# Three u tiles side by side at the start of a hybrid GLA and S5 block, with their weights laid out by the host

## The chip, the cores and the metric

The program runs on one core of a Trainium2 chip. The metric is the device time of one execution in microseconds (us); the time before is the median of three runs. The engines are TensorE (PE; its weight loads are PEld), VectorE (DVE), ScalarE (ACT), GpSimd (POOL) and SyncE (SP), which here only starts transfers.

## What is computed

One decoder block on 512 tokens and 16 meta tokens of width 1024. RMSNorm, then one wide projection `w_in` whose columns feed two mixers: gated linear attention (q, k, v, r, a) and a grouped diagonal state-space layer S5 (u). Gates mix both, then follow an output projection and a squared-ReLU MLP, each with a norm around it. The prologue, which the change is about, computes `u` and the normed input:

```python
xn = rmsnorm(h, g_mix_pre[l])          # h * rsqrt(mean(h*h) + EPS) * g
proj = xn @ w_in[l]
a_low = proj[..., R_END:A_END]
u = proj[..., A_END:U_END]             # 1024 columns, 8 tiles of 128
```

## The kernel before

Every product is made of three passes in float32r: an operand is split into a rounded part (`hi`, by ScalarE) and a remainder (`lo`, by VectorE), and TensorE adds hi x hi, hi x lo and lo x hi into one bank of PSUM. The contraction over 1024 is in 8 steps `k` of 128, so one weight tile of 128 columns against one token group is 24 matmuls. The tokens are cut into two halves of 256 and 272 (`HALVES`).

The norm's factor per token isn't known when the first bytes are in. So the prologue multiplies the *raw* tokens, scaled by the norm vector g alone (`taken_raw`: `rh` by ScalarE, `rl` by VectorE, from the transposed tokens `xT`, which the host provides in two pieces `x_cols0` and `x_cols1`), and applies the factor to the results (`u_took`, `scale_rows`). Tiles 0 to 4 of u go this way; the words below call their weights w0 to w4.

- Five warm-up matmuls (`busy(5)`) run on constants.
- ScalarE's queue starts the transfers of g and of the first quarters (two k) of w0 and w1, then loads its function table. SP's queue starts slices of x and the rest of w0 and w1 in the order of the list at L475, then the second half of x, `ab`, w2, the tokens by rows (`xt`) and the further weights. An issue may wait for the landing of an earlier transfer; the transfers of one queue go in order.
- `side_by_side` multiplies w0 and w1 against the first half, k by k, w0's three passes and then w1's; then the same against the second half. Then comes w2 alone against the first half, with `spread(0)` before its fourth k, w2 against the second half, w3 with `spread(1)` before its fourth k, w3 and w4.
- `squared` and `rooted` make the factor `xrs` from the tokens by rows. `spread` turns it into rows with a few small float32 matmuls; `rows_of` (ScalarE) copies these out. All that VectorE does next hangs on it: `u_took` of the first results, `scaled` (x times factor), `low` (remainder of the normed tokens, `xl`), in between the remainders of w3 and w4, and at the end `wa`, the weights of `a_low`.
- Then `low_rank` is the first product on the normed tokens (`mm<-xh,wa`); from there on the dense tiles follow one by one, each with weights prepared two slots ahead.

In the prologue the orders of TensorE, VectorE and ScalarE are those of the code (`keep_in_program_order`). Weight buffers (`wraw`, `whi`, `wlo`) are three deep.

Of the kernel before, what the change touches and what calls it, by code (L numbers as in the profile page):

```python
# [44 lines left out]
NBLK = GRP // GB  # L45

C_Q, C_K, C_V, C_R, C_A, C_U, C_ZG, C_ZS = 0, 512, 1024, 2048, 3072, 3088, 4112, 5136


@with_exitstack  # L50
def hybrid_block(ctx: ExitStack, tc: tile.TileContext, io, out: bass.AP):
# [406 lines left out]
    V.memset(ones, 1.0)  # L458
    g8 = mk(pxt, [P, KT], tag="g8")
    nc.scalar.dma_start(g8, io["g_cols"])  # L460
    xT = mk(pxt, [P, KT, NT], tag="xT")
    rh, rl = (mk(pxt, [P, KT, LINE + SEQ], F32R, tag=t)[:, :, :NT] for t in ("rh", "rl"))
    raws, xts, loaded = [mk(wp, [P, KT, P], tag="wraw", bufs=3) for _ in range(2)], {}, None

# [3 lines left out]
    def first_w(queue, i, k, n):  # L468
        return queue.dma_start(raws[i][:, k : k + n], w_in[k * P : (k + n) * P, C_U + i * P : C_U + (i + 1) * P].rearrange("(k p) n -> p k n", p=P))

    first_w(nc.scalar, 0, 0, 2)
    held = first_w(nc.scalar, 1, 0, 2)
    with tc.issue_after(held.ins):
        S.activation(warm, warm, AF.Sqrt)
    for i, k, n in (("x", 0, 1), ("x", 1, 1), (0, 2, 2), ("x", 2, 2), (1, 2, 2), ("x", 4, 2), (0, 4, 4), (1, 4, 4), ("x", 6, 2)):  # L475
        with behind():
            if i == "x":
                loaded = nc.sync.dma_start(xT[:, k : k + n, :256], io["x_cols0"][:, k : k + n])
            else:
                loaded = first_w(nc.sync, i, k, n)  # L480
    idle = bank()
# [12 lines left out]
    early = []  # L494
    for kind, i in (("h", 0), ("h", 4), ("a", 0), ("u", 2), ("x", 0), ("x", 1), ("x", 2), ("x", 3), ("x", 4), ("u", 3), ("u", 4), ("w", 0), ("g", 0), ("u", 5), ("c", 0), ("u", 6), ("u", 7)):
        with behind():
            if kind == "x":
                loaded = x_load(i)
            elif kind == "h":
                loaded = nc.sync.dma_start(xT[:, i : i + 4, 256:], io["x_cols1"][:, i : i + 4])  # L500
            elif kind == "a":
                loaded = nc.sync.dma_start(ab, io["a_step"])
            elif kind == "w":
                wraw = mk(pg, [P, KT, 16], tag="waraw")
                loaded = nc.sync.dma_start(wraw, w_in[:, C_A : C_A + 16].rearrange("(k p) n -> p k n", p=P))
            elif kind == "g":
                wgu = scratch()[:96].rearrange("p a b -> p (a b)")
                loaded = nc.sync.dma_start(wgu, io["w_gates"])
            elif kind == "c":
                for dst, src in ((CA, io["c_cols"][0]), (CB, io["c_cols"][1]), (BA, io["b_cols"][0])):  # L510
                    loaded = nc.sync.dma_start(dst.rearrange("p g h -> p (g h)"), src)
            else:
                loaded, raw = raw_w(w_in[:, C_U + i * P : C_U + (i + 1) * P])
                raws.append(raw)
# [73 lines left out]

    def side_by_side(ws, q, pss):
        a, b = HALVES[q]  # L590
        for k in range(KT):
            for (hi, lo), ps in zip(ws, pss):
                for i, (w, t) in enumerate(((hi, rh), (hi, rl), (lo, rh))):
                    PE.matmul(ps[:, : b - a], w[:, k], t[:, k, a:b], start=(k == 0 and i == 0), stop=(k == KT - 1 and i == 2))

# [4 lines left out]
    uts = [u_tile() for _ in range(3)] + [mk(qc, [P, T8, NCK], tag=f"ut{i}") for i in (3, 4)]  # L600
    busy(5)
    w0, w1 = (tuple(mk(wp, [P, KT, P], F32R, tag=t, bufs=3) for t in ("whi", "wlo")) for _ in range(2))
    for k in range(KT):
        taken_raw(k, 0)
        for w, raw in zip((w0, w1), raws):
            if k in (0, 2):
                split_part(w, raw, slice(k, k + 2))
            elif k == 4:
                split_part(w, raw, slice(k, KT))
    firsts = bank("mm"), bank()  # L610
    side_by_side((w0, w1), 0, firsts)
    for k in range(KT):
        taken_raw(k, 1)
    last = {0: bank("mm"), 1: bank("mm")}
    side_by_side((w0, w1), 1, (last[0], last[1]))
    w2_ = split_w(raws[2])
    squared(0)
# [5 lines left out]
    squared(2)  # L623
    pair2, spreads = bank("mm"), []
    raw_product(w2_, 0, pair2, (3, lambda: spreads.append(spread(0))))
    rows_of(0, spreads[0])
# [9 lines left out]
    high(0, range(0, 4))  # L636
    last[2] = bank()
    raw_product(w2_, 1, last[2])
    low(0, (0, 2))
    raw_product(w3, 0, pair2[:, 256:], (3, lambda: spreads.append(spread(1))))  # L640
    w4_hi = split_w_hi(raws[4])
# [3 lines left out]
    low(0, (4, 6))  # L645
    last[3] = bank()
    raw_product(w3, 1, last[3])
    last[4] = bank()
# [1352 lines left out]
def laid_out(np, given):  # L2001
# [11 lines left out]
    tokens = np.concatenate([a["x"][0], a["meta_tokens"]]).T.reshape(8, P, NT).transpose(1, 0, 2)  # L2013
    rows["x_cols0"], rows["x_cols1"] = tokens[:, :, :256], tokens[:, :, 256:]
    rows["w_gates"] = np.concatenate([a["w_gate_up"][0]] * 6)
    rows["g_cols"] = a["g_mix_pre"][0].reshape(8, P).T
    return {**{name: a[name] for name in _INS}, **rows}
# [26 lines left out]
```

## Time and profile before

| what | value |
|---|---|
| median of 3 runs | 860.62 us (860.51 to 862.09) |
| the profiled execution's own time | 861.4 us |
| its span, first to last instruction | 859.7 us |
| TensorE busy | 849.5 us, 99% |
| VectorE busy | 680.2 us, 79% |
| ScalarE busy | 465.0 us, 54% |

Times in the profile are us from the first instruction. A row of the timeline has start, length, engine, line, operation and tiles (`out<-in`); in brackets stands how long the engine was idle before it and who released it. The length of a matmul is modelled and longer than its spacing, so spacings are read from starts. L61, L66 and L79 are helpers through which all matmuls and the ordered instructions go; the tile's name tells them apart.

### The profile page before, as it was taken

What the parts mean: (1) busy time and instruction counts of PE and PEld (TensorE: products, weight loads), DVE (VectorE), ACT (ScalarE), POOL (GpSimd) and SP (SyncE); (2) the same over time, 40 slices, a digit from 0 to 9 for tenths busy, and PEclk for the clock granted to TensorE, in tenths of its full rate; (3) what the DMA queues carried; (4) which work ended last, traced back from release to release, by engine and by line L of the source; (5) the groups of instructions that cost most, each with busy time, mean ns of one, the idle gap of its engine ahead of it and who ended that gap; (6) DMA issues with size and microseconds to landing.
All of it is one profiled execution on the core that took longest, in us unless ns stands there. A gap on an engine that the chain in (4) does not pass through costs nothing.

```text
span 859.7 us, 13744 instructions
## 1 busy us (share of the span) xinstructions
PE 849.5 (99%) x4952; PEld 726.6 (85%) x4952; DVE 680.2 (79%) x1264; ACT 465.0 (54%) x816; POOL 151.1 (18%) x265
## 2 busy tenths in 40 slices
PE   9999999999999999999999999999999999999996
PEld 8998899898988888888888889988888888888885
DVE  6999889988787499856888788667666777688886
ACT  7677466676764455335454466433222246885763
POOL 1123120140303222341121421011121100000001
PEclk9999999999999999999999999999999999999998
DMA  9887775566465856977788896498989967866564
GB/s 313 194 281 225 224 143 146 147 174 168 115 156 154 241 156 149 257 202 270 233 271 266 270 294 196 147 323 291 360 262 343 352 223 234 278 195 196 172 199 144
DMA packets 172491, 192.66 MB, mean 224 GB/s; under 512 B 18648, under 2 KB 127352, under 8 KB 172424
## 3 DMA queue, kind: packets, MB, share of 16 engines
q1 hardware_dynamic: 145040, 109.66, 45.1%
q0 software_dynamic: 25408, 77.93, 27.2%
q10 hardware_dynamic: 1976, 4.20, 1.6%
q8 instruction: 39, 0.64, 0.3%
q14 instruction: 28, 0.23, 0.1%
HBM read 149.52 MB, written 42.24 MB: 223 GB/s over the span
## 4 chain that ended last, share of the span: by engine, by line
PE 52%; issue 2%; POOL 1%; DMA 1%; DVE 1%; ACT 0%; DVEq 0%; POOLq 0%
PE mm L61 36%; PE sm L61 16%; DMA qi<-qd 1%; POOL M L1178 0%; PE sm L66 0%; POOL td L1277 0%; DVE c L1964 0%; POOL qd L1250 0%; DVE c L1938 0%; POOL qi L1448 0%; DVE gl L1450 0%; DVEq L2040 0%; ACT gh L164 0%; DMA kpad<-krow 0%; DVE ff_r L150 0%
## 5 line engine op out<-in xcount | busy, mean ns | idle before, releaser
L164 ACT ACTIVATE whi<-wraw 128x1024 fp32r<-128x1024 f32 x81 | 85.8, 1059 | 181.1 <-PE mm L61 177.6
L179 DVE TENSOR_TENSOR wlo<-wraw,whi 128x1024 fp32r<-128x1024 f32 x81 | 99.1, 1225 | 79.0 <-ACT whi L164 77.2
L61 PE MATMUL mm<-xh,whi 128*128 128x512 f32 (+2 forms) x464 | 158.5, 342 | 0.0
L61 PE MATMUL mm<-xh,wlo 128*128 128x512 f32 (+2 forms) x464 | 155.5, 335 | 0.0
L61 PE MATMUL mm<-xl,whi 128*128 128x512 f32 (+2 forms) x464 | 155.4, 335 | 0.0
L61 PE MATMUL mm<-hh,whi 128*128 128x512 f32 (+1 forms) x272 | 100.9, 371 | 0.0
L61 PE MATMUL mm<-hl,whi 128*128 128x512 f32 (+1 forms) x272 | 100.8, 371 | 0.0
L61 PE MATMUL mm<-hh,wlo 128*128 128x512 f32 (+1 forms) x272 | 100.8, 371 | 0.0
L61 PEld LDWEIGHTS mm<-xh,whi 128*128 128x128 f32 x464 | 87.4, 188 | 9.7 <-issue 1.0
L61 PEld LDWEIGHTS mm<-xh,wlo 128*128 128x128 f32 x464 | 87.4, 188 | 9.0
L61 PEld LDWEIGHTS mm<-xl,whi 128*128 128x128 f32 x464 | 87.4, 188 | 8.4
L1881 DVE TENSOR_TENSOR wlo<-wraw,whi 128x1024 fp32r<-128x1024 f32 x56 | 68.4, 1223 | 21.4 <-ACT whi L1877 21.3
L61 PE MATMUL sm<-wlo,fh 128*128 128x512 f32 x192 | 74.9, 390 | 0.0
L61 PE MATMUL sm<-whi,fl 128*128 128x512 f32 x192 | 74.8, 390 | 0.0
L61 PE MATMUL sm<-whi,fh 128*128 128x512 f32 x192 | 74.8, 389 | 0.0
L1877 ACT ACTIVATE whi<-wraw 128x1024 fp32r<-128x1024 f32 x56 | 58.7, 1050 | 15.5 <-PE mm L61 11.7
L61 PEld LDWEIGHTS mm<-hh,whi 128*128 128x128 f32 x272 | 51.3, 189 | 8.8
L61 PEld LDWEIGHTS mm<-hh,wlo 128*128 128x128 f32 x272 | 51.3, 189 | 8.7
L61 PEld LDWEIGHTS mm<-hl,whi 128*128 128x128 f32 x272 | 51.3, 189 | 8.6
L164 ACT ACTIVATE fh<-f 128x512 fp32r<-128x512 f32 x48 | 30.2, 629 | 36.8 <-PE sm L61 23.0
L61 PE MATMUL mm<-gl,whi 128*128 128x512 f32 x128 | 50.0, 390 | 0.1
L61 PE MATMUL mm<-gh,whi 128*128 128x512 f32 x128 | 49.9, 390 | 0.0
(490 smaller groups left out, 1863.2 us busy)
## 6 DMA issues: line engine op xcount, KB each, us to landing
wraw<-in_w_ff_dram SPq DMA_DIRECT2D x56, 512.0 KB, 7.5
wraw<-in_w_in_dram SPq DMA_DIRECT2D x46, 512.0 KB, 5.6
w2raw<-in_w_ff_dram POOLq DMA_DIRECT2D x16, 1024.0 KB, 9.0
t2d<-w2t POOLq DMA_DIRECT2D x16, 1024.0 KB, 6.3
wraw<-t2d SPq DMA_DIRECT2D x32, 512.0 KB, 4.2
wraw<-in_w_glu_dram SPq DMA_DIRECT2D x16, 512.0 KB, 5.2
M<-kpad POOLq DMA_DIRECT2D x64, 64.0 KB, 2.6
wraw<-in_w_o_gla_dram SPq DMA_DIRECT2D x8, 512.0 KB, 7.4
```

The costliest lines, as they stand in the source:

```text
L61: ins = nc.tensor.matmul(*args, **kw)
L164: return S.activation(dst, src, AF.Copy, scale=scale)
L179: V.tensor_sub(lo, raw, f32(hi))
L1877: halved = S.activation(bh, raw, AF.Copy)
L1881: V.tensor_sub(bl, raw, f32(bh))
```

## The change

- `FIRST = 3`: the first three tiles run side by side in both halves. For each k the pass is now the outer loop and the tile the inner one. w2's separate products go away, and so does its separate split.
- The host lays the three tiles out as `w_first`, for each tile one line of 4 KB per partition; a transfer of two k moves 1 KB per partition, one of four k 2 KB, where it moved pieces of 512 B out of `w_in`.
- The norm vector and the first slice of x are one array `g_x_cols` and one transfer into one tile `gx`; g's own transfer goes. `xT` and `g8` are views of that tile.
- The list of first transfers has w2 in it, x comes as 1, 1, 2 and 4 k, and the second half of x as 2 and 6 k (it was 4 and 4).
- Four warm-ups in place of five.
- `spread(0)` now stands before the sixth k of the three tiles' second half, and `spread(1)` before the third k of w3's second half.

```diff
     pxt = pool("pxt", stack=sx, padded=True)
     ones = mk(pxt, [P, 256], tag="ones")
     V.memset(ones, 1.0)
-    g8 = mk(pxt, [P, KT], tag="g8")
-    nc.scalar.dma_start(g8, io["g_cols"])
-    xT = mk(pxt, [P, KT, NT], tag="xT")
+    gx = mk(pxt, [P, KT + KT * NT], tag="gx")
+    g8, xT = gx[:, :KT], gx[:, KT:].rearrange("p (k t) -> p k t", t=NT)
     rh, rl = (mk(pxt, [P, KT, LINE + SEQ], F32R, tag=t)[:, :, :NT] for t in ("rh", "rl"))
-    raws, xts, loaded = [mk(wp, [P, KT, P], tag="wraw", bufs=3) for _ in range(2)], {}, None
+    raws, xts, loaded = [mk(wp, [P, KT, P], tag="wraw", bufs=3) for _ in range(FIRST)], {}, None
 
     def behind():
         return tc.issue_after(loaded.ins) if loaded else ExitStack()
 
     def first_w(queue, i, k, n):
-        return queue.dma_start(raws[i][:, k : k + n], w_in[k * P : (k + n) * P, C_U + i * P : C_U + (i + 1) * P].rearrange("(k p) n -> p k n", p=P))
+        return queue.dma_start(raws[i][:, k : k + n], io["w_first"][i][:, k : k + n])
 
     first_w(nc.scalar, 0, 0, 2)
     held = first_w(nc.scalar, 1, 0, 2)
     with tc.issue_after(held.ins):
         S.activation(warm, warm, AF.Sqrt)
-    for i, k, n in (("x", 0, 1), ("x", 1, 1), (0, 2, 2), ("x", 2, 2), (1, 2, 2), ("x", 4, 2), (0, 4, 4), (1, 4, 4), ("x", 6, 2)):
+    for i, k, n in (("x", 0, 1), (2, 0, 2), ("x", 1, 1), (0, 2, 2), (1, 2, 2), ("x", 2, 2), (2, 2, 2), (0, 4, 4), ("x", 4, 4), (1, 4, 4), (2, 4, 4)):
         with behind():
-            if i == "x":
-                loaded = nc.sync.dma_start(xT[:, k : k + n, :256], io["x_cols0"][:, k : k + n])
+            if i != "x":
+                loaded = first_w(nc.sync, i, k, n)
+            elif k:
+                loaded = nc.sync.dma_start(xT[:, k : k + n, :256], io["x_cols0"][:, k - 1 : k - 1 + n])
             else:
-                loaded = first_w(nc.sync, i, k, n)
+                loaded = nc.sync.dma_start(gx[:, : KT + 256], io["g_x_cols"])
...
     early = []
-    for kind, i in (("h", 0), ("h", 4), ("a", 0), ("u", 2), ("x", 0), ("x", 1), ("x", 2), ("x", 3), ("x", 4), ("u", 3), ("u", 4), ("w", 0), ("g", 0), ("u", 5), ("c", 0), ("u", 6), ("u", 7)):
+    for kind, i in (("h", 0), ("h", 2), ("a", 0), ("x", 0), ("x", 1), ("x", 2), ("x", 3), ("x", 4), ("u", 3), ("u", 4), ("w", 0), ("g", 0), ("u", 5), ("c", 0), ("u", 6), ("u", 7)):
         with behind():
             if kind == "x":
                 loaded = x_load(i)
             elif kind == "h":
-                loaded = nc.sync.dma_start(xT[:, i : i + 4, 256:], io["x_cols1"][:, i : i + 4])
+                loaded = nc.sync.dma_start(xT[:, i : 3 * i + 2, 256:], io["x_cols1"][:, i : 3 * i + 2])
...
-    def side_by_side(ws, q, pss):
+    def side_by_side(ws, q, pss, within=None):
         a, b = HALVES[q]
         for k in range(KT):
-            for (hi, lo), ps in zip(ws, pss):
-                for i, (w, t) in enumerate(((hi, rh), (hi, rl), (lo, rh))):
-                    PE.matmul(ps[:, : b - a], w[:, k], t[:, k, a:b], start=(k == 0 and i == 0), stop=(k == KT - 1 and i == 2))
+            if within and k == within[0]:
+                within[1]()
+            for i, (part, t) in enumerate(((0, rh), (0, rl), (1, rh))):
+                for w, ps in zip(ws, pss):
+                    PE.matmul(ps[:, : b - a], w[part][:, k], t[:, k, a:b], start=(k == 0 and i == 0), stop=(k == KT - 1 and i == 2))
 
...
-    busy(5)
-    w0, w1 = (tuple(mk(wp, [P, KT, P], F32R, tag=t, bufs=3) for t in ("whi", "wlo")) for _ in range(2))
+    busy(4)
+    ws_ = [tuple(mk(wp, [P, KT, P], F32R, tag=t, bufs=3) for t in ("whi", "wlo")) for _ in range(FIRST)]
     for k in range(KT):
         taken_raw(k, 0)
-        for w, raw in zip((w0, w1), raws):
+        for w, raw in zip(ws_, raws):
             if k in (0, 2):
                 split_part(w, raw, slice(k, k + 2))
             elif k == 4:
                 split_part(w, raw, slice(k, KT))
-    firsts = bank("mm"), bank()
-    side_by_side((w0, w1), 0, firsts)
+    firsts, pair2, spreads = (bank("mm"), bank()), bank("mm"), []
+    side_by_side(ws_, 0, (*firsts, pair2[:, :256]))
     for k in range(KT):
         taken_raw(k, 1)
-    last = {0: bank("mm"), 1: bank("mm")}
-    side_by_side((w0, w1), 1, (last[0], last[1]))
-    w2_ = split_w(raws[2])
     squared(0)
     squared(1)
     V.tensor_copy(tri, trif)
@@ -621,8 +622,8 @@
     rooted(slice(0, 2))
     work(1.3)
     squared(2)
-    pair2, spreads = bank("mm"), []
-    raw_product(w2_, 0, pair2, (3, lambda: spreads.append(spread(0))))
+    last = {0: bank("mm"), 1: bank("mm"), 2: bank()}
+    side_by_side(ws_, 1, (last[0], last[1], last[2]), (5, lambda: spreads.append(spread(0))))
     rows_of(0, spreads[0])
     for i in range(2):
         u_took(firsts[i][:, :256], uts[i], 0, True)
@@ -634,17 +635,15 @@
     rooted(slice(2, TT + 1))
     scaled(0, range(6, 8))
     high(0, range(0, 4))
-    last[2] = bank()
-    raw_product(w2_, 1, last[2])
     low(0, (0, 2))
-    raw_product(w3, 0, pair2[:, 256:], (3, lambda: spreads.append(spread(1))))
+    raw_product(w3, 0, pair2[:, 256:])
+    last[3] = bank()
+    raw_product(w3, 1, last[3], (2, lambda: spreads.append(spread(1))))
...
-    last[3] = bank()
-    raw_product(w3, 1, last[3])
...
     tokens = np.concatenate([a["x"][0], a["meta_tokens"]]).T.reshape(8, P, NT).transpose(1, 0, 2)
-    rows["x_cols0"], rows["x_cols1"] = tokens[:, :, :256], tokens[:, :, 256:]
+    rows["x_cols0"], rows["x_cols1"] = tokens[:, 1:, :256], tokens[:, :, 256:]
     rows["w_gates"] = np.concatenate([a["w_gate_up"][0]] * 6)
-    rows["g_cols"] = a["g_mix_pre"][0].reshape(8, P).T
+    rows["g_x_cols"] = np.concatenate([a["g_mix_pre"][0].reshape(8, P).T, tokens[:, 0, :256]], axis=1)
+    rows["w_first"] = a["w_in"][0][:, C_U : C_U + FIRST * P].reshape(KT, P, FIRST, P).transpose(2, 1, 0, 3)
```

SP's queue, from the program's start: before (`xT` is x, `wraw_49` is w0, `wraw_50` is w1, `wraw_52` is w2).

```order
L478 DMA xT_46_149<-in_x_cols0_dram 128x256 x2
L469 DMA wraw_49_152<-in_w_in_dram 128x2x128
L478 DMA xT_46_149<-in_x_cols0_dram 128x2x256
L469 DMA wraw_50_153<-in_w_in_dram 128x2x128
L478 DMA xT_46_149<-in_x_cols0_dram 128x2x256
L469 DMA wraw_49_152<-in_w_in_dram 128x4x128
L469 DMA wraw_50_153<-in_w_in_dram 128x4x128
L478 DMA xT_46_149<-in_x_cols0_dram 128x2x256
L500 DMA xT_46_149<-in_x_cols1_dram 128x4x272 x2
L502 DMA ab_20_116<-in_a_step_dram 128x192
L170 DMA wraw_52_170<-in_w_in_dram 128x8x128
```

And with the change (`gx` is x, `wraw_48`, `49` and `50` are w0, w1 and w2; ScalarE's queue starts the first quarters of w0 and w1 in both).

```order
L482 DMA gx_45_147<-in_g_x_cols_dram 128x264
L469 DMA wraw_50_152<-in_w_first_dram 128x256
L480 DMA gx_45_147<-in_x_cols0_dram 128x256
L469 DMA wraw_48_150<-in_w_first_dram 128x256
L469 DMA wraw_49_151<-in_w_first_dram 128x256
L480 DMA gx_45_147<-in_x_cols0_dram 128x2x256
L469 DMA wraw_50_152<-in_w_first_dram 128x256
L469 DMA wraw_48_150<-in_w_first_dram 128x512
L480 DMA gx_45_147<-in_x_cols0_dram 128x4x256
L469 DMA wraw_49_151<-in_w_first_dram 128x512
L469 DMA wraw_50_152<-in_w_first_dram 128x512
L502 DMA gx_45_147<-in_x_cols1_dram 128x2x272
```

All of w2 now goes ahead of the second half of x (`x_cols1`), where it came behind it; a row of 128x256 is 128 KB.

TensorE at the start of the first half: before, the warm-ups and the first k (`whi_74`, `wlo_75` of w0, `whi_76`, `wlo_77` of w1).

```order
L61 MATMUL sm_51_166<-ones_44_145 128x256 x5
L61 MATMUL mm_78_250<-rh_47_150,whi_74_218 128x256
L61 MATMUL mm_78_250<-rl_48_151,whi_74_218 128x256
L61 MATMUL mm_78_250<-rh_47_150,wlo_75_219 128x256
L61 MATMUL sm_79_251<-rh_47_150,whi_76_220 128x256
L61 MATMUL sm_79_251<-rl_48_151,whi_76_220 128x256
L61 MATMUL sm_79_251<-rh_47_150,wlo_77_221 128x256
```

And with the change (`whi_73`, `75` and `77` are those of w0, w1 and w2, `wlo_74`, `76` and `78` their remainders).

```order
L62 MATMUL sm_51_167<-ones_44_145 128x256 x4
L62 MATMUL mm_79_256<-rh_46_148,whi_73_216 128x256
L62 MATMUL sm_80_257<-rh_46_148,whi_75_218 128x256
L62 MATMUL mm_81_258<-rh_46_148,whi_77_220 128x256
L62 MATMUL mm_79_256<-rl_47_149,whi_73_216 128x256
L62 MATMUL sm_80_257<-rl_47_149,whi_75_218 128x256
L62 MATMUL mm_81_258<-rl_47_149,whi_77_220 128x256
L62 MATMUL mm_79_256<-rh_46_148,wlo_74_217 128x256
L62 MATMUL sm_80_257<-rh_46_148,wlo_76_219 128x256
L62 MATMUL mm_81_258<-rh_46_148,wlo_78_221 128x256
```

The third row of every k now needs w2, and the first remainder `wlo` is wanted in the seventh place.

TensorE around `spread(0)`: before, inside w2 alone (`mm_86`) against the first half.

```order
L61 MATMUL mm_86_393<-rh_47_150,whi_82_366 128x256
L61 MATMUL mm_86_393<-rl_48_151,whi_82_366 128x256
L61 MATMUL mm_86_393<-rh_47_150,wlo_83_368 128x256
L61 MATMUL sm_87_403<-ident_3_78,xrs_66_202 128x128 x2
L61 MATMUL mm_86_393<-rh_47_150,whi_82_366 128x256
L61 MATMUL mm_86_393<-rl_48_151,whi_82_366 128x256
L61 MATMUL mm_86_393<-rh_47_150,wlo_83_368 128x256
```

And with the change, inside the three tiles' second half (`mm_84`, `mm_85`, `sm_86`).

```order
L62 MATMUL mm_84_370<-rh_46_148,wlo_74_217 128x272
L62 MATMUL mm_85_371<-rh_46_148,wlo_76_219 128x272
L62 MATMUL sm_86_372<-rh_46_148,wlo_78_221 128x272
L62 MATMUL sm_87_418<-ident_3_78,xrs_65_201 128x128 x2
L62 MATMUL mm_84_370<-rh_46_148,whi_73_216 128x272
L62 MATMUL mm_85_371<-rh_46_148,whi_75_218 128x272
L62 MATMUL sm_86_372<-rh_46_148,whi_77_220 128x272
```

In front of it stand 45 matmuls of 272 columns of that half, where there were the whole half of two tiles (48) and 9 of w2.

## Rows read from the trace of the kernel before

**Rows 1.** The page, part 1: busy time, share, instructions of TensorE.
```profile
PE 849.5 (99%) x4952; PEld 726.6 (85%) x4952; DVE 680.2 (79%) x1264; ACT 465.0 (54%) x816; POOL 151.1 (18%) x265
```

**Rows 2.** Waits of TensorE, whole run: us in total, times, longest us.
```profile
PE sm L61 <- DVE xss L517: 1.3, 1, 1.3
...
```

**Rows 3.** Timeline of TensorE, first half; then one window: us, busy, clock, DMA.
```profile
1.31 4.16 PE L61 MATMUL sm<-ones 128*128 128x256 f32 x10 [1.31 <-DVE xss L517]
...
10.40 0.39 PE L61 MATMUL sm<-rh,whi 128*128 128x256 f32 x1 [0.32 <-ACT whi L79]
10.62 0.28 PE L61 MATMUL sm<-rl,whi 128*128 128x256 f32 x1
11.12 0.39 PE L61 MATMUL sm<-rh,wlo 128*128 128x256 f32 x1 [0.22 <-DVE wlo L79]
...
11.86 0.28 PE L61 MATMUL sm<-rh,whi 128*128 128x256 f32 x1
...
13.55 0.28 PE L61 MATMUL mm<-rh,whi 128*128 128x272 f32 x1
...
5.20:13.55 8.35, 7.63 (x50) 1.00 1.07 345
```

**Rows 4.** Timeline of ScalarE, where it waits for transfers in the prologue.
```profile
4.73 0.42 ACT L79 ACTIVATE whi<-wraw 128x256 fp32r<-128x256 f32 x1 [0.57 <-DMA wraw<-in_w_in_dram]
5.63 0.42 ACT L79 ACTIVATE whi<-wraw 128x256 fp32r<-128x256 f32 x1 [0.49 <-DMA wraw<-in_w_in_dram]
...
9.72 0.63 ACT L79 ACTIVATE whi<-wraw 128x512 fp32r<-128x512 f32 x1 [0.80 <-DMA wraw<-in_w_in_dram]
...
12.27 3.42 ACT L79 ACTIVATE rh<-xT,g 128x272 fp32r<-128x272 f32 x8 [0.60 <-DMA xT<-in_x_cols_dram]
15.60 1.04 ACT L79 ACTIVATE whi<-wraw 128x1024 fp32r<-128x1024 f32 x1
```

**Rows 5.** VectorE behind spread(0): one window, then its last row.
```profile
21.86:37.32 15.46, 15.36 (x36) 1.00 1.01 233
...
37.03 0.29 DVE L79 TENSOR_TENSOR wa<-waraw,wa 128x128 fp32r<-128x128 f32 x1
```

**Rows 6.** Timeline of TensorE around spread(0), spread(1) and at low_rank.
```profile
20.54 0.61 PE L61 MATMUL sm<-ident,xrs 128*128 128x128 f32 x4
20.90 0.37 PE L61 MATMUL mm<-rh,whi 128*128 128x256 f32 x1
...
26.60 0.28 PE L61 MATMUL mm<-rh,wlo 128*128 128x256 f32 x1
27.02 1.00 PE L61 MATMUL sm<-ident,xrs 128*128 128x128 f32 x6
27.95 0.39 PE L61 MATMUL mm<-rh,whi 128*128 128x256 f32 x1
...
38.52 0.28 PE L61 MATMUL mm<-xh,wa 128*32 128x256 f32 x1
```

**Rows 7.** Transfers in 7 to 8, 11 to 12 and 16 to 17 us.
```profile
DMA packets 627, 0.31 MB, mean 314 GB/s; under 512 B 19, under 2 KB 627, under 8 KB 627
...
DMA packets 363, 0.39 MB, mean 388 GB/s; under 512 B 5, under 2 KB 363, under 8 KB 363
...
DMA packets 119, 0.42 MB, mean 422 GB/s; under 512 B 16, under 2 KB 16, under 8 KB 119
```

**Rows 8.** Timeline of VectorE, the remainder of w1's second half.
```profile
10.38 0.69 DVE L79 TENSOR_TENSOR wlo<-wraw,whi 128x512 fp32r<-128x512 f32 x1 [0.74 <-ACT whi L79]
```

**Rows 9.** Waits of VectorE from 21.5 to 104 us, all of them.
```profile
DVE wlo L79 <- ACT whi L79: 0.5, 2, 0.3
DVE wgr L79 <- ACT wgr L79: 0.2, 1, 0.2
```

**Rows 10.** Timelines of VectorE and TensorE at 82 us.
```profile
81.11 1.20 DVE L79 TENSOR_TENSOR wlo<-wraw,whi 128x1024 fp32r<-128x1024 f32 x1
...
82.65 0.39 PE L61 MATMUL mm<-xh,wlo 128*128 128x512 f32 x1
```

More of the change, by code (lines that the diff above doesn't have):

```diff
@@ L45 @@
 NBLK = GRP // GB
+FIRST = 3
 C_Q, C_K, C_V, C_R, C_A, C_U, C_ZG, C_ZS = 0, 512, 1024, 2048, 3072, 3088, 4112, 5136
```

## The prediction

> **What bounds the kernel now.** I read the page first, then the waits of TensorE, then the start of the run on each engine. TensorE is busy for 849.5 of 859.7 us [rows 1], and the list of what TensorE waited for over the whole run has four entries, the longest the 1.3 us shown, the others at most 0.3 [rows 2]. So the time falls only if TensorE gets through the prologue sooner, and if nothing later makes it wait for what was gained.
>
> In the prologue the first token half runs from 5.20 to 13.55 us, 8.35 us [rows 3]. Its 48 matmuls of 256 columns are spaced 0.113 us when nothing is missing (15 of them from 11.86 to 13.55), which would be 5.4 us. The rows at 10.40 and 11.12 name what is missing: the rounded weights `whi` and their remainder `wlo`. Behind them stands the transfer: ScalarE sat idle for 0.80 us until the second half of weight tile 1 had landed, and took it up at 9.72 [rows 4]. So TensorE waits for ScalarE, which waits for bytes. Behind the first half TensorE is dense, but VectorE is close behind it: from 21.86 to 37.32 us VectorE works 15.36 of 15.46 us without a break and ends with `wa` [rows 5], which TensorE wants at 38.52 [rows 6].
>
> **The change part by part.** *Three tiles in the first half.* The first half grows from 48 to 72 matmuls and the 24 that w2 had later go away. The work is the same; the point is to fill holes with it. Without the change, the equal point (all 72 done) is 13.55 plus 24 matmuls of w2. At 0.113 these are 2.7 us: 16.3 us.
>
> When are they done with the change? The weights' second halves are asked for in the order w0, x, w1, w2, and one row of TensorE's order behind the first matmul of each k needs w2. Ahead of the end of w2's second half the queues carry 2564 KB (ScalarE's 256, and 2308 on SP's queue by the order shown above; 128x256 elements are 128 KB). Before, 1792 KB were in by 9.72 and 2592 KB by 12.27 [rows 4]. On that line, (2564-1792)/800 x 2.55 + 9.72 = 12.2 us: the late end.
>
> *The host's layout.* All of w's rows were 512 B; now they are 1 and 2 KB. What row size is worth in this prologue can be read from three stretches of one us [rows 7]: 314 GB/s in a stretch of 627 packets averaging about 0.5 KB, 388 in one of 363 of about 1.1 KB, 422 in one of 119 of about 3.5 KB. I anchor at the weights of tile 1 that ScalarE took at 5.63, behind 640 KB [rows 4]; the change has 644 KB by the like point, which I leave at 5.6. The other 1920 KB (1.966 MB) then take 4.7 us at 422, 5.1 at 388, 6.3 at 314: landing at 10.3, 10.7 or 11.9. I take 10.7, since the pieces are 1 and 2 KB and half of them are still slices of x in 1 KB rows; the ends are 10.3 and 12.2.
>
> The Trainium skill speaks against this part: in "DMA: Bandwidth & Descriptors", section Specifications, it puts the smallest transfer for line rate at 512 B, so that longer rows would bring nothing. By that rule the sum keeps the 12.2. The trace does not agree: 314 against 388 GB/s.
>
> From landing to the end of the half: ScalarE rounds w2 (0.63, the row at 9.72), VectorE subtracts (0.69 [rows 8]), with about 0.13 for three hand-overs; the first matmul behind a wait is spaced 0.22 (10.40 to 10.62 [rows 3]), and 27 more of 0.113 are 3.05. Together 4.7 us, so the half ends at 15.4 against 16.3: **0.9 us gained**. The same sum from the landing at 9.72, with 18 matmuls in place of 27, gives 13.4 where the trace has 13.55.
>
> *Weights innermost* (`side_by_side`): the remainder `wlo` is wanted as the seventh of nine and no longer as the third of three, which covers VectorE's 0.69; I count it only in that wait.
>
> *The norm vector with x, ScalarE's list one DMA shorter.* ScalarE gets to its table load one DMA issue earlier, but then waits for the first slice and for weights, as at 4.73 and 5.63 [rows 4]. Nothing on the path; a loss is excluded only as far as the first slice (4 KB longer) doesn't land later than the weights behind it.
>
> *One warm-up less* takes 0.83 us (4.16 for five [rows 3]) out of the time ahead of the first product. The first weights are rounded at 5.15 (4.73 + 0.42), so the four that are left, done at about 4.7, end in idle time: price nothing, unless the clock suffers (below).
>
> *spread(1)* moves behind 21 more matmuls. There TensorE's spacing was 0.42 ahead of the six small matmuls and 0.93 over them, where four cost 0.36 at 20.54 [rows 6]: some 0.7 us of waiting for `xrs`, now covered by products. And `w2`'s split leaves ScalarE's and VectorE's lists between the halves and goes into the first half.
>
> **Where it stalls next.** The three-tile second half puts spread(0) 45 matmuls of 272 columns in, 45 x 0.1234 = 5.55 us behind 15.4: at **21.0** in place of 20.54. Its input is in time: before, ScalarE's path from the first rounding of the second half (12.27) to spread(0) took 8.3 us with 1.04 for w2 in it [rows 4, 6]; without w2 it is 7.2, and the last slices land near 10.7 + 1.114 MB at 388 GB/s = 13.6, so it ends by 20.8 even if it began only then. But `rows_of(0)` hangs on spread(0), and all of VectorE's unbroken stretch on that: `wa` comes 16.8 us behind spread(0) (37.32 less 20.54 [rows 5, 6]), at 37.8. TensorE alone would be there at 38.5 - 0.9 - 0.7 = 36.9. So VectorE sets it, and of 1.6 us **0.7** are left.
>
> VectorE stays on the heels of TensorE. It has three idle spots up to 104 us, 0.5 us behind `whi` in two and 0.2 behind `wgr` [rows 9]. I give back 0.5 of these 0.7, where ScalarE stands behind products that TensorE now has earlier, and leave 0.2 for a weight's landing, which the change doesn't hurry. At 82.65 TensorE wants a `wlo` that VectorE finished at 82.31 (81.11 + 1.20): slack 0.34, less 0.05 for the hand-over [rows 10]. VectorE, 0.45 later at spread(0) and 0.5 recovered, is there about 0.05 earlier: TensorE can be at most 0.35 earlier. That is the tightest place I found. **Net: about 0.4 us faster.** The profiled execution took 861.4 (its span and 1.7 around it), so 861.0; it lay 0.8 above the median of 860.62, which becomes 860.2.
>
> **The rivals.** *Late bytes: the layout buys nothing* (the change doesn't do what it says). For it: the stretches of long rows all lie later in the run than those of short ones, so the time of the run could be what differs. w2 lands at 12.2, 1.5 later than in my sum: the half ends at 16.9, spread(0) at 22.5, and the same chain through VectorE makes 1.1 us of loss: 861.7. It turns into a loss from a landing at about 11.1.
>
> *VectorE isn't the bound after all*: were its stretch to start or run sooner, TensorE's own 1.6 us stay: 859.0, and 858.6 with a landing at 10.3. Against it: the 15.36 of 15.46 us, in an order that the change keeps.
>
> *Slower: TensorE stays at its slow level through the first half.* The warm-ups ran 0.42 us for each of ten records of 256 columns [rows 3], where the four records of 128 columns at 20.54 took 0.36 together [rows 6], 0.09 each: some half pace, the 1.2 of the two levels 1.2 and 2.4 GHz. From 5.20 to 13.55 the granted clock is 1.00 [rows 3]. With one of five taken away the rise could come late. If all 72 matmuls went at 0.213, the half would end at 5.2 + 15.3 = 20.5, 5.1 us behind my 15.4: 865.3. It decides only if the low level lasts past the w2 wait, near 12 us; before that the matmuls wait for bytes anyhow. Against it: full spacing stands right behind the w1 waits, from 11.86 on, after a stretch that was no denser than the new one.
>
> The Trainium skill, "TensorE: Matmul & The Clock Gate", Part 1, says that the default state is throttled and that activity releases the throttle, which is this rival's mechanism. The trace agrees that the warm-ups ran at the low level; no run here yet shows fewer of them.
>
> **How the numbers follow.** My forecast, a gain of 0 to 1.1 us (landing 10.3 to 11.1, VectorE as the bound): 0.57, time 860.2. Late bytes, 861.7: 0.2. TensorE's own gain, 859.0: 0.12. Slow level, 865.3: 0.07. Something unlisted: 0.04, either way. Two tenths of a per cent, about what a measurement can tell from no change, are 1.7 us. The forecast and the late bytes lie within it; of the third case half lies beyond. Faster 0.10, same 0.79, slower 0.11. The range takes in the first three cases, and the runs of one kernel, which spread from 860.51 to 862.09: 858.8 to 862.0.
>
> **What would show it.** In the profile after: `whi` of the third tile taken up behind a wait for its weights near 10.7, and the 72nd matmul near 15.4; spread(0) near 21.0; TensorE waiting for `wlo` of w3 or for `wa` around 25 and 37.8, where it didn't wait before; the first `mm<-xh,wa` near 37.8; a short wait for `wlo` near 82. It would be wrong if the third tile's weights land before 10 or after 11.5, if spread(0) doesn't hold VectorE, if matmuls past 12 us are spaced 0.22, or if a later wait swallows what the prologue gave.

## The result and the profile after

The changed kernel takes 863.55 us (median of 8 runs, 862.98 to 865.36) where the kernel before takes 861.47 beside it (8 runs): the ratio is 1.0027, with a 95% interval from 1.0017 to 1.0036. It is **2.1 us slower**, and outside the range that I gave (858.8 to 862.0). The profiled execution took 863.5, so it stands for the median; its span is 861.8, where before it was 859.7.

From the page of the changed kernel the line of busy times, and the head of the list of what TensorE waited for (us in total, times, longest), which answer to [rows 1] and [rows 2]:

```profile
PE 849.8 (99%) x4950; PEld 726.5 (84%) x4950; DVE 680.2 (79%) x1266; ACT 465.2 (54%) x818; POOL 151.1 (18%) x265
```

```profile
PE mm L62 <- ACT whi L80: 1.7, 3, 0.6
PE sm L62 <- DVE xss L519: 1.3, 1, 1.3
PE mm L62 <- DVE wlo L80: 0.8, 1, 0.8
```

TensorE's work is the same (849.5 and 849.8 us busy). The waits for `whi` and `wlo`, the two halves of a weight, come to 2.5 us, where before had some 0.5. One of them, 0.54 us at 8.54, counts for nothing as long as the next, at 11.86, ends on a landing; the others lie at two places, which the next views show. First, ScalarE at the end of the first token half, and TensorE behind it (start us, us, engine, line, operation, out<-in; in brackets the idle time ahead and what ended it):

```profile
9.01 0.49 ACT L80 ACTIVATE rh<-gx 128x256 fp32r<-128x256 f32 x1
10.78 0.51 ACT L80 ACTIVATE rh<-gx 128x256 fp32r<-128x256 f32 x1 [1.27 <-DMA gx<-in_x_cols_dram]
11.20 1.65 ACT L80 ACTIVATE whi<-wraw 128x512 fp32r<-128x512 f32 x3
```

```profile
10.98 0.28 PE L62 MATMUL mm<-rh,wlo 128*128 128x256 f32 x1
11.86 0.38 PE L62 MATMUL mm<-rh,whi 128*128 128x256 f32 x1 [0.61 <-ACT whi L80]
12.38 0.38 PE L62 MATMUL sm<-rh,whi 128*128 128x256 f32 x1
12.90 0.38 PE L62 MATMUL mm<-rh,whi 128*128 128x256 f32 x1
...
17.08 0.41 PE L62 MATMUL mm<-rh,whi 128*128 128x272 f32 x2
```

ScalarE is idle from 9.5 to 10.78, and what ends it is no weight but x: slices 4 to 7, which the change asks for as one DMA of 512 KB ahead of the second halves of w1 and w2. Behind it stand four roundings in a row, and TensorE gets its three `whi` at 11.86, 12.38 and 12.90. The first half is over at **17.08**; the equal point of before was worked out as 16.3, and I had forecast 15.4. Here 0.8 us are lost.

Second, the end of the second token half, on TensorE, ScalarE and VectorE:

```profile
22.64 0.61 PE L62 MATMUL sm<-ident,xrs 128*128 128x128 f32 x4
...
26.30 0.28 PE L62 MATMUL sm<-rh,wlo 128*128 128x272 f32 x1
27.11 0.38 PE L62 MATMUL mm<-rh,whi 128*128 128x256 f32 x1 [0.53 <-ACT whi L80]
27.34 0.28 PE L62 MATMUL mm<-rl,whi 128*128 128x256 f32 x1
28.38 0.39 PE L62 MATMUL mm<-rh,wlo 128*128 128x256 f32 x1 [0.76 <-DVE wlo L80]
...
31.73 0.93 PE L62 MATMUL sm<-ident,xrs 128*128 128x128 f32 x6
...
40.70 0.28 PE L62 MATMUL mm<-xh,wa 128*32 128x256 f32 x1
```

```profile
26.00 1.06 ACT L80 ACTIVATE whi<-wraw 128x1024 fp32r<-128x1024 f32 x1 [1.03 <-PE mm L62]
```

```profile
27.09 1.23 DVE L80 TENSOR_TENSOR wlo<-wraw,whi 128x1024 fp32r<-128x1024 f32 x1 [0.80 <-ACT whi L80]
```

ScalarE wants to round tile 3's weights and waits 1.03 us **for TensorE**: there are three buffers each of `whi` and `wlo`, and w0, w1 and w2 hold all three until the three-tile second half is nearly over. Only then do the rounding (1.06) and the subtraction (1.23) follow, and TensorE stands still for most of 26.4 to 28.4, some 1.85 us. spread(1), at 31.73, has no wait ahead of it any more.

`mm<-xh,wa`, the first product of `low_rank`, starts at 40.70 where it was 38.52 [rows 6]: 2.18 later, and the span is 2.1 longer. So all of the loss is in the first 41 us: 0.8 from the first half, 1.85 from tile 3's split, and some 0.4 back where spread(1) waited before.

### The profile page after: what moved, and what is told of

The parts are those of the page before. It is cut to its first block, busy times and chain, and to the rows that moved or that the text cites. A ratio compares the mean times of both kernels' runs of the same rounds, so it can differ in the third digit from the quotient of the medians.

```text
span 861.8 us, 13744 instructions
## 1 busy us (share of the span) xinstructions
PE 849.8 (99%) x4950; PEld 726.5 (84%) x4950; DVE 680.2 (79%) x1266; ACT 465.2 (54%) x818; POOL 151.1 (18%) x265
## 4 chain that ended last, share of the span: by engine, by line
PE 89%; DVE 5%; DMA 3%; ACT 1%; issue 1%; SPq 0%; ACTq 0%; DVEq 0%
PE mm L62 65%; PE sm L62 23%; PE sm L67 2%; DMA ro<-og 1%; DMA gx<-in_x_cols_dram 1%; DVE wlo L180 1%; ACT whi L80 0%; DMA U<-ud 0%; DMA wraw<-in_w_first_dram 0%; DVE rs L1260 0%; DVE wlo L80 0%; DVE c L1963 0%; DVE M L80 0%; DVE ogl L1262 0%; ACTq L80 0%
## 5 line engine op out<-in xcount | busy, mean ns | idle before, releaser
L1876 ACT ACTIVATE whi<-wraw 128x1024 fp32r<-128x1024 f32 x56 | 58.7, 1049 | 16.3 <-PE mm L62 11.7
L62 PE MATMUL mm<-gh,wlo 128*128 128x512 f32 x128 | 49.8, 389 | 0.0
```

The source lines that it names most:

```text
L62: ins = nc.tensor.matmul(*args, **kw)
L1876: halved = S.activation(bh, raw, AF.Copy)
```

## The experiments

Two measures are used for every kernel: T1, where the first matmul of the second token half starts, and L, where the first `mm<-xh,wa` starts. T1 holds what the bytes do, L-T1 what the kernel does with it. Both are read from the one profiled execution of a kernel; those of e1, e6, e8 and e10 were the slowest of their runs. The time is the median of 8 to 11 runs (of 4 for e10), and beside it its difference to the median of the kernel before in the same series.

| kernel | T1 | L | L-T1 | median us | against before | highest us |
|---|---|---|---|---|---|---|
| before | 13.55 (two tiles) | 38.52 | | | | |
| changed | 17.08 | 40.70 | 23.62 | 863.55 | +2.1 | 865.36 |
| e3_no_layout | 16.73 | 40.34 | 23.61 | 863.35 | +1.7 | 864.80 |
| e13_round_w0_first | 16.75 | 40.37 | 23.62 | 862.95 | +1.8 | 865.13 |
| e10_x_last | 19.98 | 43.61 | 23.63 | 866.13 | +4.6 | 867.32 |
| e6_x_split | 15.78 | 39.40 | 23.62 | 861.98 | +0.4 | 862.51 |
| e1_own_place | 19.49 | 42.22 | 22.73 | 862.87 | +1.2 | 865.01 |
| e1b_own_place_early | 16.68 | 39.97 | 23.29 | 863.55 | +1.9 | 865.54 |
| e2_pair_second | 17.48 | 39.85 | 22.37 | 862.72 | +1.1 | 865.13 |
| e12_split_own_place | 15.75 | 38.56 | 22.81 | 860.79 | -0.4 | 862.29 |
| e11_split_and_pair | 15.44 | 37.90 | 22.46 | 860.43 | -0.7 | 860.78 |
| e4_all_but_three | 13.06 (two tiles) | 38.40 | | 861.28 | -0.3 | 862.66 |
| e8_before_spread1 | 12.72 (two tiles) | 37.52 | | 860.87 | -0.7 | 862.16 |
| e14_all_but_three_spread1 | 13.14 (two tiles) | 37.79 | | 861.04 | -0.1 | 861.97 |

The five kernels that differ in transfers or in the work of the first half alone have L-T1 of 23.61 to 23.63, whatever T1 is. So the two causes can be read apart.

### The buffers

`e1_own_place` puts the split of tile 3 elsewhere:

```diff
-    w3 = split_w(raws[3])
+    far = slice(NT - P, NT)
+    split_hi(xh[:, :, far], raws[3])
+    V.tensor_sub(xl[:, :, far], raws[3], f32(xh)[:, :, far])
+    w3 = xh[:, :, far], xl[:, :, far]
```

> The changed kernel, but the two halves of tile 3's weights (rounded, remainder) go into the last 128 columns of xh and xl, which are written only later, so they need no buffer of the three. Theory A (the loss is made of two steps: w2's bytes land at 12.0 and not at 10.7, and tile 3's weights find no free buffer until the three-tile second half is over): the rounding no longer waits for TensorE near 26.0 but starts near 25.0 when ScalarE is free; VectorE, free at 26.3, ends the remainder near 27.5, so TensorE waits once, about 0.9 us, in place of 0.5 and 0.8; the first mm<-xh,wa near 39.8 in place of 40.7, the time near 862.7, 0.9 below the changed kernel and 1.2 above before. Rival B (VectorE, held by spread(0), sets the end whatever tile 3 does): first mm<-xh,wa stays at 40.7, 863.5. Rival C (a slow clock or the bytes alone make the loss): 863.5 too, with the w3 waits gone.

Measured: 862.87, ratio 1.0014 (1.0005 to 1.0024); the wait for the rounding of tile 3 is gone, L-T1 is 0.89 less than in the changed kernel. One wait is left there, for the remainder, which now lies in `xl`:

```profile
29.90 0.39 PE L62 MATMUL mm<-rh,xl 128*128 128x256 f32 x1 [0.68 <-DVE xl L80]
```

That is theory A's size, and B (VectorE sets the end anyway) falls. But T1 itself was 19.49 in this trace, which no theory had: that is the clock, below.

`e1b_own_place_early` also moves these lines ahead of `rows_of(0)`.

> As the run before, and tile 3's split is also moved ahead of rows_of(0) on ScalarE and VectorE, into their idle time from 21.3 to 23.3 and from 22.6 to 24.0. Theory A: TensorE doesn't wait at tile 3 at all, first mm<-xh,wa near 38.9, time near 861.7, that is 1.9 below the changed kernel and 0.2 above before; what then is left of the loss is the late bytes. Rival B (VectorE sets the end): since 1.2 us of VectorE's work goes into its idle time and 0.8 of idle time goes away, even B gives up to 2.0 less if VectorE was the bound, but then the run before shows no gain. Rival C: 863.5.

Measured: 863.55, ratio 1.0021 (1.0012 to 1.003). A miss, by an oversight of mine: ScalarE's row shows that tile 3's raw weights had not landed at the new place.

```profile
23.34 1.06 ACT L80 ACTIVATE xh<-wraw 128x1024 fp32r<-128x1024 f32 x1 [2.49 <-DMA wraw<-in_w_in_dram]
24.30 0.36 ACT L80 COPY xrows<-sm 128x256 f32<-128x256 f32 x1
```

`xrows`, on which all of VectorE's stretch hangs, queued behind that wait until 24.30 (23.28 in the changed kernel, although spread(0) came 0.4 later there). TensorE had no wait at tile 3, came to `low_rank` earlier, and waited there:

```profile
39.97 0.30 PE L62 MATMUL mm<-xh,wa 128*32 128x256 f32 x1 [1.16 <-DVE wa L80]
```

So VectorE is the bound as soon as its stretch begins late, as the prediction had it; this trace is the only one in which TensorE waited for `wa`.

`e2_pair_second` frees two of the three buffers early instead:

```diff
-    side_by_side(ws_, 1, (last[0], last[1], last[2]), (5, lambda: spreads.append(spread(0))))
+    side_by_side(ws_[:2], 1, (last[0], last[1]), (7, lambda: spreads.append(spread(0))))
+    raw_product(ws_[2], 1, last[2])
```

> The changed kernel with three tiles side by side in the first half only; in the second half tiles 0 and 1 go side by side and tile 2 follows alone, as before the change, with spread(0) behind 42 of the products. The buffers of tiles 0 and 1 are then free near 23.0. Theory A: no wait for a buffer at tile 3; its rounding starts near 24.7, its remainder ends near 27.2, TensorE waits about 0.7 once; first mm<-xh,wa near 39.6, time near 862.5. Rivals B and C: 863.5.

Measured: 862.72, ratio 1.0011 (1.0003 to 1.002). L-T1 is 22.37, 1.25 less than in the changed kernel: of the 1.85 us of waiting most is gone. What is left is this wait:

```profile
27.52 0.38 PE L62 MATMUL mm<-rh,wlo 128*128 128x256 f32 x1 [0.30 <-DVE wlo L80]
```

### The bytes

`e3_no_layout` reads the weights of tiles 0 to 2 from the weight matrix as before:

```diff
-        return queue.dma_start(raws[i][:, k : k + n], io["w_first"][i][:, k : k + n])
+        return queue.dma_start(raws[i][:, k : k + n], w_in[k * P : (k + n) * P, C_U + i * P : C_U + (i + 1) * P].rearrange("(k p) n -> p k n", p=P))
```

> The changed kernel with the weights of tiles 0 to 2 read in 512 B rows from the weight matrix, as before the change, in place of the host's layout. Theory A (row size is worth nothing here, the bytes are late because of their number): w2's second half lands at 12.0 again, the 72nd matmul near 17.1, time 863.5. Rival D (the layout does raise the rate, and without it the change would have been worse; the rate of 314 against 388 GB/s in the trace of before): landing near 13.5, the 72nd matmul near 18.6, time near 865.0.

Measured: 863.35, ratio 1.0021 (1.0012 to 1.003), against the changed kernel's 1.0027. T1 was even 0.35 earlier. Two stretches of one us (us, busy of PE, PEld, DVE, ACT, POOL with instructions, clock, DMA share, GB/s), first with the layout, then without:

```profile
7.00:8.00 1.00, 1.00 (x9) 0.80 (x8) 0.00 (x0) 0.32 (x1) 0.00 (x0) 1.00 0.83 251
...
11.00:12.00 1.00, 0.39 (x4) 0.20 (x2) 0.64 (x2) 1.00 (x3) 0.00 (x0) 1.00 1.03 366
```

```profile
7.00:8.00 1.00, 0.47 (x5) 0.27 (x3) 0.29 (x1) 0.83 (x3) 0.00 (x0) 1.00 1.04 315
...
11.00:12.00 1.00, 0.38 (x1) 0.19 (x1) 0.97 (x2) 1.00 (x3) 0.00 (x0) 1.00 1.08 368
```

366 against 368 GB/s at the same place, and from 7 to 8 us the long rows were the slower ones. Over the whole stretch from 4 to 12 us it is 323 GB/s without the layout, and 291 to 322 in the five traces that have it with the same list of transfers. The kernel before, too, has a stretch of short rows beside the one of 314 GB/s that I had read [rows 7], from 13 to 14 us:

```profile
DMA packets 642, 0.36 MB, mean 365 GB/s; under 512 B 10, under 2 KB 632, under 8 KB 642
```

Rival D falls: **the host's layout brings nothing that these runs show**.

`e4_all_but_three` is the other side of it, the kernel before with the layout, the norm vector with the first slice and four warm-ups, but two tiles:

```diff
-    busy(5)
+    busy(4)
-    nc.scalar.dma_start(g8, io["g_cols"])
+                loaded = nc.sync.dma_start(gx[:, : KT + 256], io["g_x_cols"])
```

> The kernel before with the side edits alone: weights of tiles 0 and 1 laid out by the host, the norm vector in front of the first slice of x, four warm-ups; two tiles side by side as before. Theory A (the loss comes from the three tiles alone): w1's second half is taken up at 9.7 give or take 0.5, TensorE dense from about 11.1, first mm<-xh,wa at 38.5 give or take 0.5, time 861.6 as before. Rival D (the layout raises the rate): w1's second half near 9.0, time 860.9. Rival E (four warm-ups keep the clock at its slow level): matmuls spaced 0.21 beyond 11 us, time 862.5 or more.

Measured: 861.28, ratio 1.0 (0.9991 to 1.001). The three side edits together cost and bring nothing that can be told (the interval reaches some 0.9 us either way), and no matmul stayed at the slow level: from 11.25 us to T1 they are spaced 0.113.

`e6_x_split` asks for x as before the change, in two pieces with the weights between them:

```diff
-    ... (0, 4, 4), ("x", 4, 4), (1, 4, 4), (2, 4, 4)):
+    ... ("x", 4, 2), (0, 4, 4), (1, 4, 4), (2, 4, 4), ("x", 6, 2)):
```

> The changed kernel with the last four slices of x in two DMAs as before the change, slices 4 and 5 ahead of the second halves of the weights, 6 and 7 behind them, in place of one 512 KB DMA. So far TensorE took up the second half of the products 1.08 us behind the landing of that DMA in each of four traces (landing 10.42, 10.78, 11.18, 11.58). Theory A: slices 4 and 5 land near 9.5, the wait is now for the weights of tiles 0, 1 and 2 in turn, the third of these matmuls starts near 12.5 in place of 12.9, the 72nd near 16.7, time near 863.1, and the waiting is broken up, so that no run is above 864.5. Rival (the sum of the bytes decides, the pieces don't): 72nd near 17.1, 863.5.

Measured: 861.98, ratio 1.0003 (0.9994 to 1.0012): 1.6 us of the 2.1 are gone with this one line. In the profiled execution L is 1.3 earlier, and so is T1: 15.78, where theory A had some 16.7. ScalarE and TensorE, to be read against their first views in the result:

```profile
9.10 0.51 ACT L80 ACTIVATE rh<-gx 128x256 fp32r<-128x256 f32 x1 [0.23 <-DMA gx<-in_x_cols_dram]
9.78 1.94 ACT L80 ACTIVATE whi<-wraw 128x512 fp32r<-128x512 f32 x3 [0.16 <-DMA wraw<-in_w_first_dram]
```

```profile
10.46 0.38 PE L62 MATMUL mm<-rh,whi 128*128 128x256 f32 x1
11.11 0.39 PE L62 MATMUL sm<-rh,whi 128*128 128x256 f32 x1 [0.27 <-ACT whi L80]
11.77 0.39 PE L62 MATMUL mm<-rh,whi 128*128 128x256 f32 x1 [0.27 <-ACT whi L80]
...
15.78 0.41 PE L62 MATMUL mm<-rh,whi 128*128 128x272 f32 x2
```

ScalarE takes slice 4 at 9.10 and then each weight as it comes; the third `whi` serves TensorE at 11.77 and not at 12.90. I had expected 12.5. There are 256 KB less ahead of w2, and by the completion events of the DMAs in the traces its second half landed at 11.06 here and at 12.04 in the changed kernel.

`e13_round_w0_first` leaves the transfers and only lets ScalarE round w0's second half ahead of slice 4.

```diff
     for k in range(KT):
+        if k == 4:
+            split_part(ws_[0], raws[0], slice(k, KT))
         taken_raw(k, 0)
```

> The changed kernel, same DMAs, but ScalarE and VectorE split the second half of tile 0's weights (landed near 9.4) ahead of slice 4 of x and not behind it. It separates the landing of the 512 KB DMA from what ScalarE does in a row behind it (0.51 for x and three times 0.52 to 0.55 for the weights). If the row on ScalarE counts: first of these matmuls 0.5 behind the landing of x in place of 1.08, the third 1.6 in place of 2.1, first mm<-xh,wa 0.5 earlier for the same landing, time near 863.0. If only the landing counts: 863.5.

Measured: 862.95, ratio 1.0023 (1.0014 to 1.0032). Its ScalarE took up slice 4 at 10.58, T1 was 16.75: 6.17 from the one to the other, where the changed kernel has 6.30 (10.78 to 17.08). So taking one rounding out of the row is worth 0.13 us, not 0.5: with it shortened, w2's landing (11.9) is next. What is late is the bytes, not ScalarE.

### One long wait, and the clock

`e10_x_last` puts the 512 KB behind all weights: `(0, 4, 4), (1, 4, 4), (2, 4, 4), ("x", 4, 4)`.

> The changed kernel with the 512 KB DMA of the slices 4 to 7 of x asked for last, behind the second halves of all three weights: the same bytes, one long wait. Expected by all theories: landing near 12.2, TensorE idle from about 10.9 to 13.2, 72nd matmul near 18.2 if the clock stays up. Clock theory (in the trace with the longest wait so far, 2.2 us up to 12.66, the granted clock was 0.50 from 14.9 to 18.0, in those with 1.85 and less it was 1.00): matmuls spaced 0.21 for some 3 us behind the wait, another 1.6 us, time 866 in most runs. Without it: 864.6.

Measured: 866.13, ratio 1.0058 (1.0044 to 1.0072), 4 runs, as the clock theory had it. The windows (clock is the third number from the end), first of this kernel, then of `e1_own_place`, whose T1 had been out of line:

```profile
10.90:13.00 2.10, 0.16 (x2) 0.00 (x0) 0.24 (x1) 0.78 (x2) 0.00 (x0) 1.00 1.11 366
15.00:18.00 3.00, 3.00 (x16) 3.00 (x16) 3.00 (x9) 3.00 (x9) 0.00 (x0) 0.50 1.02 406
```

```profile
10.90:12.60 1.70, 0.00 (x0) 0.00 (x0) 0.47 (x1) 1.02 (x3) 0.00 (x0) 1.00 1.07 390
14.90:18.00 3.10, 3.10 (x16) 3.10 (x16) 3.08 (x9) 2.77 (x7) 0.00 (x0) 0.50 1.04 408
```

In both, TensorE stood still for over 2 us (10.78 to 13.30, and 10.49 to 12.66), took up the matmuls, those of them that waited for nothing at first still spaced 0.11 to 0.13 us, and was then granted 0.50, the 1.2 GHz level, for some 3 us in which matmuls are spaced 0.213: 16 of them cost 1.6 us. In the other twelve traces, that of the changed kernel among them, the clock is 1.00 throughout 14.9 to 18.0; the longest standstill of the same kind there, 1.85 us, is in e2 (10.41 to 12.26). That its executions above 865 are such cases is likely, not shown: there is no trace of them. What speaks for it is the last column of the table: the kernels with the 512 KB DMA reach 864.8 to 867.3, those with split slices 860.8 to 862.5.

### Both causes away, and the parts that are left

`e12_split_own_place` (the edits of e6 and e1) and `e11_split_and_pair` (those of e6 and e2):

> The changed kernel with split slices of x and tile 3's weight halves in the unused columns of xh and xl, so with the three-tile second half kept. Buffer theory: no wait for the rounding of tile 3 near 25, one shorter wait for its remainder, first mm<-xh,wa near 38.6 in place of 39.4, time near 861.2. If it is not the buffers but the place of the split in ScalarE's list that makes the wait: 39.4 and 862.0.

> The changed kernel with both supposed causes taken away: the last slices of x in two DMAs (as in the run with split slices), and tiles 0 and 1 side by side, then tile 2, in the second half (as in the run with the pair). If the two effects add: the split alone brought the first mm<-xh,wa from 40.70 to 39.40; the pair, read against the landing of x in its own trace, 1.2 more, so 38.2 and a time of 860.8 to 861.2, at or just below before. If VectorE takes over as the bound (wa at 38.72 in the run with split slices): TensorE waits for wa, 39.0, 861.7.

Measured: 860.79, ratio 0.9999 (0.999 to 1.0008), and **860.43, ratio 0.9991 (0.9982 to 1.0)**. L-T1 is 22.81 and 22.46, within 0.1 of e1 and e2 without the split: the effects add. In e12 the split of tile 3 keeps its place in ScalarE's list and only its buffers change, so it is the buffers that make the wait and not the place in the list. In e11, ScalarE takes up w2 and TensorE ends the half and reaches `low_rank` as follows:

```profile
10.74 0.63 ACT L80 ACTIVATE whi<-wraw 128x512 fp32r<-128x512 f32 x1 [0.35 <-DMA wraw<-in_w_first_dram]
```

```profile
15.44 0.41 PE L62 MATMUL mm<-rh,whi 128*128 128x272 f32 x2
...
37.90 0.28 PE L62 MATMUL mm<-xh,wa 128*32 128x256 f32 x1
```

`e8_before_spread1` is the kernel before with spread(1) alone moved, `e14_all_but_three_spread1` the same with the side edits of e4.

```diff
-    raw_product(w3, 0, pair2[:, 256:], (3, lambda: spreads.append(spread(1))))
+    raw_product(w3, 0, pair2[:, 256:])
+    last[3] = bank()
+    raw_product(w3, 1, last[3], (2, lambda: spreads.append(spread(1))))
```

> The kernel before with one part of the change alone: spread(1) moved from the first to the second product of tile 3, 21 matmuls later. By the term of the prediction (0.7 us of waiting for xrs covered, VectorE done with wa at 37.32): no wait ahead of the six small matmuls, first mm<-xh,wa near 37.8 in place of 38.5, time near 861.0, 0.7 below before. Rival (rows_of(1) comes later by as much, and scaled(1) on VectorE with it, so that wa is what TensorE waits for): first mm<-xh,wa at 38.5 or later behind a wait for wa, time 861.7.

> Every part of the change but the three tiles side by side: host's layout (tiles 0 and 1), norm vector with the first slice, four warm-ups, spread(1) in tile 3's second product; products and transfers else as before. The two runs that hold its parts gave 861.28 and 860.87 beside 861.54 of before; if they add, first mm<-xh,wa near 37.4 and a time of 860.6, the best of all; if VectorE's wa (36.9 in both) holds TensorE, 37.3 and the same; if the parts disturb each other, 861.5.

Measured: 860.87, ratio 0.9997 (0.9988 to 1.0005), and 861.04, ratio 0.9998 (0.9989 to 1.0007). Neither can be told from before by its interval. In the traces L is 37.52 and 37.79, 1.0 and 0.7 earlier than before; of e8's 1.0 the earlier T1 is 0.8. TensorE waits neither for `wa` nor for `xrs`. Counted from spread(0), `low_rank` comes after 17.98 us before and 18.35 in e4, after 17.82 in e8 and 17.66 in e14: the move brings 0.2 in the one pair and 0.7 in the other. e4, without the move, shows the wait that the move takes away:

```profile
26.89 1.00 PE L61 MATMUL sm<-ident,xrs 128*128 128x128 f32 x6 [0.51 <-DVE xrs L79]
```

The six small matmuls and what follows them, in e8:

```profile
28.55 0.93 PE L61 MATMUL sm<-ident,xrs 128*128 128x128 f32 x6
29.41 0.39 PE L61 MATMUL sm<-rh,whi 128*128 128x272 f32 x1
```

Without any wait they take 0.86, where before they took 0.93 [rows 6].

e8's profiled run took 862.16, since TensorE waited at another place, which the list of its waits names:

```profile
PE mm L61 <- ACT gh L164: 1.2, 1, 1.2
```

That is at 399 us, behind a `gh` for which ScalarE had waited for a transfer (`qi<-qd`); e14's trace has 0.7 us of the same wait and e10's 0.8, the other eleven, those of before and of e11 among them, have none. What the prologue wins can be lost there, as it falls; an early arrival isn't the cause by itself, since e10 comes there latest of all.

Not run by themselves are the order of the passes in `side_by_side` and the second half of x as 2 and 6 k. e11 has both and isn't slower than before.

## Why the prediction was wrong

- **The landing of w2, 10.7: wrong, and with it the end of the half.** I had both ends, 10.3 and 12.2; it was 12.0, behind the 11.5 that I had named as a sign of being wrong. The step that failed is the rate that I gave to longer rows, read from three stretches of different times [rows 7]. At the same time of the run, from 11 to 12 us, there are 368 GB/s without the layout and 366 with it, and the kernel before moved packets of some 0.56 KB at 365 GB/s from 13 to 14 us, so short rows are not what made the stretch at 314 slow. The rival "late bytes" had that right. Whether the 422 GB/s come from the time of the run, as it said, or from packets of some 3.5 KB, no run separates. The Trainium skill, "DMA: Bandwidth & Descriptors", section Specifications, whose 512 B for line rate I had set aside on account of that row, is borne out by e3 and e4; here the page was right and my reading of the row was not.
- **What holds TensorE at the end of the half: missed.** I followed w2 and not the 512 KB of x ahead of it, though the new list of DMAs stood in the change. From landing to the end of the half the sum of 4.7 us holds: 4.7 in e6, e11 and e12 (10.72 to 15.44 in e11); with the x in one piece 5.0. So of the 1.7 us between 15.4 and 17.08, 1.3 are w2's landing and 0.3 what ScalarE's roundings behind x add, of which e13 gave back 0.13.
- **Late bytes alone: 1.1 us of loss, 861.7.** This rival had the half's end at 16.9 and spread(0) at 22.5; they were 17.08 and 22.64. It was right up to there; I had given it 0.2.
- **The buffers: left out.** The rest of the loss, some 1 us, is the wait of tile 3's split for one of three buffers. In no term or rival did I ask who frees `whi` and `wlo`. I had "TensorE waiting for `wlo` of w3" among the things to look for, but as an effect of a late VectorE. The runs put the buffers' price at 0.8 (e12 against e6, median and L-T1), and the whole place at 1.2 (e11 against e6).
- **spread(1) covered, 0.7 us: right in kind, too large.** No wait stands ahead of it in any kernel with the edit. But I had counted part of the 0.93 over the six small matmuls as waiting, from four that cost 0.36, and six cost 0.86 without a wait. What was to be had in the trace of before was the 0.3 ahead of them and 0.07; in e4's trace, where they came later behind spread(0) (6.84 us for 6.48), it was 0.7.
- **VectorE behind spread(0): right as a mechanism** (e1b), but in the changed kernel it decided nothing: `wa` was done at 40.32, and TensorE came for it at 40.70.
- **The side edits at nothing, and the slow level through the first half: right and rightly rejected** (e4). In the changed kernel's profile the first products are spaced 0.21 to 0.22 up to 6.53 us, as under the 0.50 of e10, and 0.11 to 0.12 from 6.69 on. The clock column reads 1.00 there, as it does over the half-pace warm-ups, so in these first us the spacing tells the level, and the 1.00 that I quoted [rows 3] would not have shown a late rise. It cost nothing that counts: from 7.8 to 8.54 TensorE stood waiting anyhow. The clock did fall later, in the two traces with the longest waits; whether a fifth warm-up would have prevented that, no run shows.
- **The tightest place at 82.65: not decisive.** No trace lists a wait of TensorE between 70 and 100 us; those of e8 and e14 gave time back at 399 us.

e11, the kernel without the two omissions, ends the half at 15.44 (15.4 forecast), reaches `low_rank` at 37.90 (37.8) and is 0.7 us below its before (0.4 forecast). That it comes so close is partly luck. w2 lands at 10.72 there with 256 KB fewer ahead of it than in my sum, not by longer rows. And what arrives at 37.90 is TensorE, 1.0 later than the 36.9 that I had given it alone, to find `wa` done since 37.51; the smaller gain at spread(1) and what is left of the wait at tile 3 both go that way. A price of 0.7 us is itself at the edge of what can be told from no change.

## What to carry to other kernels

When a change keeps more things alive side by side, list for each pool who holds its buffers and until when; a wait that TensorE ends on ScalarE is the sign of it. Follow the transfers in the order in which they are asked for, and put no large piece in front of small ones that are wanted as soon: the piece that is waited for need not be the one that was added. A rate is compared at the same time of the run, by a kernel that differs in nothing else.

## What was not expected of the hardware

- With the same list of DMAs ScalarE took up the same 512 KB of x between 10.37 and 11.58 us (10.37, 10.42, 10.58, 10.78, 11.18, 11.58 in six traces, the second without the layout). Because TensorE waits for it, this scatter goes straight into the time: T1 lies 6.30 or 6.31 us behind it in the four of these traces that have neither e13's edit nor the slow clock.
- In the two traces in which TensorE stood still for 2.2 and 2.5 us, its granted clock was 0.50 for some 3 us, and not at once: the matmuls were spaced 0.213 from 14.97 and 14.98 on, 2.3 and 1.7 us after the work had been taken up at 12.66 and 13.30. At 16 matmuls this cost some 1.6 us. The Trainium skill, "TensorE: Matmul & The Clock Gate", Part 1, has it that the throttled level is the default and activity releases it; the two traces agree in that a standstill came ahead of the fall.
- A transfer near 400 us (`qi<-qd`) lands with a scatter large enough to make TensorE wait 0.7, 0.8 or 1.2 us in three executions, and not at all in the other eleven.
